# Residual and final norm weights loaded into a finished input ring, and softmax scaling by whole tiles, in the second mixer of a two-layer RWKV-7 / NSA block

## The chip, the cores and the metric

The kernel runs as one program on one core of a Trainium2 chip. The metric is device microseconds of one execution, taken as the median of several runs; lower is better. Everything is float32 outside, and matrix products are made from float32r parts (below).

## What is computed

A sequence of 256 tokens with 2048 channels goes through two layers. The first is an RWKV-7 mixer, the second a sparse-attention mixer (NSA) that reads keys and values made once from the first layer's output. Cut to what the change touches:

```python
h = h + y                                     # after the first mixer; y is its output
shared = nsa_shared_kv(h, kv_norm_g, kv_w, cmp_pe, cmp_w1, cmp_w2)
u = rmsnorm(h, b_norm_g)
proj = u @ w_in                               # 16 heads of q, 3 gates for each head, z
gates = sigmoid(gl)
s = (q . k) * d ** -0.5                       # for compressed, selected, windowed keys
p = softmax(where(visible, s, NEG_INF))       # times "any key visible" for the compressed ones
o = gb[0] * o_cmp + gb[1] * o_sel + gb[2] * o_win
h = h + (o * silu(z)) @ w_o                   # the last product, 2048 x 2048
return rmsnorm(h, final_g)
```

With 256 tokens every selected block and every windowed key is inside the causal triangle, so one head needs, for its two halves of 128 query tokens, a score tile of 128x800: 15 compressed keys and the causal keys of two kinds of key (selected and windowed).

## The kernel before, in words

**Weights.** All weight matrices stream through one class, `Weights`. SyncE (SP) loads a piece of 512 KB into one of five raw buffers (tile `wraw`, L176). ScalarE (ACT) rounds a unit of 128x512 to its high part `whi` (L204), and VectorE (DVE) subtracts to get the low part `wlo` (L189). In the last 144 units before the output projection, every third low part is made by GpSimd (POOL) instead. A product of two such numbers takes three matmuls: high by high, high by low, low by high. One raw piece holds two units, so a unit of 128x512 feeds six matmuls (L568, L569, L571) for the two halves of tokens. The high and low buffers are five deep, and the code asks for units three ahead.

**Rings.** The split input of each product lives in a ring of 16 buffers of 128x512 float32r; one buffer holds the high and the low part of 128 channels by 256 tokens. Ring `mx1` holds the normalized input `u` of the second mixer, which its query, gate and z products read. Ring `mx0` holds the attention's gated output `ob`.

**The second mixer.** `QZ` is the order in which five query blocks (`phase_q`) and sixteen z blocks (`phase_z`) of the input projection run on TensorE (PE). The last one is the z block of head 0. Beside them a generator, `attn_all`, works through the eight pairs of heads, from the last pair to the first. For a head, `weigh` makes scores on PE, adds masks, takes the maximum, takes exponentials on ACT with their sums, and scales the probabilities by gate over sum on DVE; for a pair, `attend` transposes the scaled probabilities on PE (L232 of the helper that records with a rank), splits them and multiplies them with the values. `flush` multiplies by z on POOL (L1622) and makes the two parts of `ob` (ACT L1624, POOL L1625).

**The output projection.** `phase_bo` multiplies `ob` with the last weight in column blocks of 512: `nb` = 0, 1, 2, then two blocks of 256. Block 0 takes the rows from 15 down to 0, since the pairs of heads come in that order. After each block `accumulate` adds the residual to the result (DVE L1658), squares it with a sum (ACT L1660) and multiplies it by the weights of the last norm (POOL L1661). The residual is the first layer's output, which was stored in DRAM as `hd`. Between block 0 and its `accumulate` stands `open_fin`: it releases the attention's memory (`at.release()`), and in the place of that memory it allots `fg` (1 MB, the norm's weights on all partitions) and `h2` (2 MB, the residual, tile `h` in the profile), and loads both.

**PSUM.** Block 0 of the output projection uses banks 2 and 0. From `open_fin` on the turn is 2, 3, 0, 1, so the first tile of block 1 goes to bank 2 again, which block 0's first `accumulate` has to read before.

**Order.** The code is run once as a Python generator program with a rough clock `sch.t` (a `yield` of a number lets at least that many ns of that clock go by before the generator goes on). The Tile scheduler then places instructions on each engine's queue by its own simulation. Each queue is worked off in order, so an instruction that waits holds back all behind it on its engine; SP's DMA issues are such a queue too.

Of the kernel before, what the change touches and what calls it, by code (L numbers as in the profile page):

```python
# [10 lines left out]
F32 = mybir.dt.float32  # L11
# [12 lines left out]
NCMP = 15  # L24
GRP = 4
# [190 lines left out]
def hybrid_kernel(ctx: ExitStack, tc: tile.TileContext, a: dict, out: bass.AP):  # L216
# [1165 lines left out]
    def compress(j, o):  # L1382
# [17 lines left out]
        if j == 0:  # L1400
            for m in range(2):
                PE.matmul(o2[:60, :128], hs[:, m, :], cw2[:, m, :], start=m == 0, stop=m == 1)
            kc = kvp.tile([128, 1, 1, 128], F32, name="kc", bufs=1)
            V.memset(kc, 0.0)
            S.activation(kc[:60, 0, 0, :], o2[:60, :128], AF.Copy)
            rope(kc, 1, C("ccos"), C("csin"), kvp, V)
            yield 0.0
            o3 = accp("tp")
            PE.transpose(o3[:, :60], kc[:60, 0, 0, :], ident[:60, :60])
            V.tensor_copy(KT[:, :, 0:NCMP], o3[:, :60].rearrange("p (g c) -> p g c", g=GRP))  # L1410
# [26 lines left out]
    gat = at.tile([128, 2, 48], F32, name="gat")  # L1437
    RST = at.tile([128, T], F32, name="RST")
    pr = accp("PT")
    for tt in range(2):  # L1440
# [9 lines left out]
    def phase_q(n):  # L1450
# [48 lines left out]
    def weigh(h):  # L1499
# [21 lines left out]
        vc = sc[:, 0:544].rearrange("p (x c) -> p x c", x=2)[:, :, 0:NCMP]  # L1521
        V.tensor_tensor(vA, vA, cb, op=OP.add)
        V.tensor_tensor(vc, vc, C("vis").rearrange("p (x c) -> p x c", x=2), op=OP.add)
        V.tensor_reduce(mx[:, 0, 0:2], vA, axis=AX.X, op=OP.max)
        V.tensor_reduce(mx[:, :, 2], vc, axis=AX.X, op=OP.max)
        V.tensor_tensor(vD, vD, cb, op=OP.add)
        V.tensor_reduce(mx[:, 1, 0:2], vB, axis=AX.XY, op=OP.max)
        V.tensor_scalar(mx, mx, -SCALE, None, op0=OP.mult)
        yield 500.0
        P0 = at.tile([128, 2, 128], F32, name="P0", bufs=PB)  # L1530
        P1 = at.tile([128, 2, 256], F32, name="P1", bufs=PB)
        Pc = at.tile([128, 2, 16], F32, name="Pc", bufs=2)
        Pcc = PCC[h // 2 % 2][:, h % 2]
        for x in range(2):
            S.activation(P0[:, x], vA[:, x], AF.Exp, scale=SCALE, bias=mx[:, 0, x:x + 1], accum_out=sm[:, 0, x:x + 1])
        for t in range(2):
            S.activation(Pc[:, t, 0:NCMP], vc[:, t], AF.Exp, scale=SCALE, bias=mx[:, t, 2:3], accum_out=sm[:, t, 2:3])
        for x in range(2):
            S.activation(P1[:, x].rearrange("p (s t) -> p s t", s=2), vB[:, x], AF.Exp, scale=SCALE,
                         bias=mx[:, 1, x:x + 1], accum_out=sm[:, 1, x:x + 1])  # L1540
# [5 lines left out]
        V.tensor_tensor(rc[:, :, 1], rc[:, :, 1], gv[:, :, 2], op=OP.mult)  # L1546
        V.tensor_tensor(rc[:, :, 2], rc[:, :, 2], gv[:, :, 0], op=OP.mult)
        yield 600.0
        for x in range(2):
            V.tensor_scalar(P0[:, x], P0[:, x], rc[:, 0, x:x + 1], None, op0=OP.mult)  # L1550
            V.tensor_scalar(P1[:, x], P1[:, x], rc[:, 1, x:x + 1], None, op0=OP.mult)
        for t in range(2):
            V.tensor_scalar(Pcc[:, t, 0:3, 0:NCMP], Pc[:, t, None, 0:NCMP].to_broadcast([128, 3, NCMP]),
                            rc[:, t, 2:3], None, op0=OP.mult)
# [86 lines left out]
        sch.run(phase_q(ph) if ph < 10 else phase_z(ph - 10))  # L1641

    def open_fin():
        nonlocal fg, h2, fin
# [5 lines left out]
        nc.sync.dma_start(fg, bass.AP(tensor=a["final_g"].tensor, offset=a["final_g"].offset, ap=[[0, 128], [1, D]]))  # L1650
# [3 lines left out]
    fg = h2 = fin = None  # L1654

    def accumulate(tt, ps, c0, cols, i):
        hv = h2[:, tt, c0:c0 + cols]
        V.tensor_tensor(hv, ps, hv, op=OP.add)  # L1658
# [74 lines left out]
```

## Time and profile before

| what | value |
|---|---|
| median of 3 runs | 1185.26 us (1180.89 to 1186.52) |
| the profiled execution's own time | 1179.32 us |
| span of its instructions | 1177.5 us |
| mean granted TensorE clock | 0.987 |
| busy share: PE, DVE, ACT, POOL | 95%, 73%, 60%, 30% |
| attention and input projection of the second mixer | about 849 to 1098 us |
| output projection | about 1067 to 1164 us |

The profile is of one execution. Busy times of PE are of pipelined matmuls, so a busy PE may still be issuing at less than its peak. "a <- b" in the waits means that a stood idle until b was done. Lines are those of the kernel before.

### The profile page before, as it was taken

How to read it: one execution, taken by the hardware profiler on the slowest of the kernel's cores; microseconds unless marked ns; L12 is line 12 of the kernel's file. 1: busy time of each engine (PE TensorE's matmuls, PEld its weight loads, DVE VectorE, ACT ScalarE, POOL GpSimd, SP SyncE). 2: the span in 40 equal slices, each digit the busy share in tenths (PEclk: the TensorE clock that was granted, in tenths of full speed). 3: DMA queues.
4: the chain of work that ended last, by engine and by line, in shares of the span. 5: the costliest groups of instructions: out<-in, count | busy, mean ns of one | idle time of the engine just before them, and what ended most of it. 6: DMA issues, size and time to landing. Idle time of an engine off the chain costs nothing.

```text
span 1177.5 us, 25042 instructions
## 1 busy us (share of the span) xinstructions
PE 1119.6 (95%) x9136; PEld 967.0 (82%) x9136; DVE 862.5 (73%) x1915; ACT 708.1 (60%) x1680; POOL 348.3 (30%) x437
## 2 busy tenths in 40 slices
PE   8999999999986999999989999999999999999797
PEld 6788899887966888888668888787889888888687
DVE  7999876589795886666656867674576888987464
ACT  5667877667763445554545766564656666656453
POOL 1400046234554355544010010100344434342211
PEclk9999999999997999999989999999999999999899
DMA  6559887786889769784356758585646354644652
GB/s 226 170 182 258 228 226 220 229 220 185 262 237 201 193 163 264 181 227 121 122 162 208 248 165 285 162 286 171 187 143 172 113 138 115 159 133 161 233 193 105
DMA packets 232922, 225.37 MB, mean 191 GB/s; under 512 B 51429, under 2 KB 180757, under 8 KB 232416
## 3 DMA queue, kind: packets, MB, share of 16 engines
q1 hardware_dynamic: 228000, 219.01, 62.7%
q0 software_dynamic: 4800, 4.77, 1.7%
q8 instruction: 72, 1.18, 0.4%
q14 instruction: 50, 0.41, 0.1%
HBM read 200.48 MB, written 23.10 MB: 190 GB/s over the span
## 4 chain that ended last, share of the span: by engine, by line
PE 69%; DVE 15%; issue 5%; ACT 4%; POOL 3%; DMA 3%; SPq 0%; ACTq 0%; POOLq 0%; DVEq 0%
PE bank L569 12%; PE bank L571 12%; PE bank L568 12%; PE bank L587 5%; PE bank L588 4%; DVE wlo L189 4%; PE bank L589 4%; PE bank L593 2%; PE bank L232 2%; PE bank L594 1%; PE pair L571 1%; PE pair L568 1%; ACT whi L204 1%; PE pair L569 1%; DVE invX L803 1%
## 5 line engine op out<-in xcount | busy, mean ns | idle before, releaser
L189 DVE TENSOR_TENSOR wlo<-wraw,whi 128x512 fp32r<-128x512 f32 (+2 forms) x616 | 444.3, 735 | 138.5 <-ACT whi L204 136.0
L204 ACT ACTIVATE whi<-wraw 128x512 fp32r<-128x512 f32 (+2 forms) x664 | 399.9, 620 | 186.2 <-PE bank L571 98.3
L569 PE MATMUL bank<-wlo,mx 128*128 128x512 f32 (+3 forms) x608 | 232.1, 383 | 6.4 <-DVE wlo L189 6.2
L571 PE MATMUL bank<-whi,mx 128*128 128x512 f32 (+3 forms) x608 | 229.6, 380 | 0.0
L568 PE MATMUL bank<-whi,mx 128*128 128x512 f32 (+3 forms) x608 | 205.8, 382 | 8.7 <-DVE h L1658 5.9
L587 PE MATMUL bank<-mx,whi 128*128 128x256 f32 (+1 forms) x544 | 166.1, 305 | 0.3 <-ACT mx L418 0.3
L589 PE MATMUL bank<-mx,wlo 128*128 128x256 f32 (+1 forms) x544 | 155.4, 286 | 0.4 <-DVE wlo L189 0.4
L588 PE MATMUL bank<-mx,whi 128*128 128x256 f32 (+1 forms) x544 | 155.3, 285 | 0.3 <-issue 0.3
L568 PEld LDWEIGHTS bank<-whi,mx 128*128 128x128 f32 x608 | 114.7, 190 | 28.2 <-DVE h L1658 6.3
L569 PEld LDWEIGHTS bank<-wlo,mx 128*128 128x128 f32 x608 | 115.7, 190 | 25.9 <-DVE wlo L189 8.4
L571 PEld LDWEIGHTS bank<-whi,mx 128*128 128x128 f32 x608 | 115.6, 190 | 17.9 <-POOL mx L1625 0.4
L587 PEld LDWEIGHTS bank<-mx,whi 128*128 128x128 f32 (+1 forms) x544 | 103.5, 190 | 5.7 <-ACT mx L418 0.7
L588 PEld LDWEIGHTS bank<-mx,whi 128*128 128x128 f32 (+1 forms) x544 | 103.9, 191 | 1.4 <-issue 0.5
L589 PEld LDWEIGHTS bank<-mx,wlo 128*128 128x128 f32 (+1 forms) x544 | 103.4, 190 | 1.7 <-DVE wlo L189 0.6
L189 POOL TENSOR_TENSOR wlo<-wraw,whi 128x512 fp32r<-128x512 f32 (+2 forms) x48 | 63.1, 1314 | 115.6 <-ACT whi L204 94.2
L593 PE MATMUL bank<-mx,whi 128*128 128x512 f32 x240 | 86.6, 398 | 0.0
L569 PE MATMUL bank<-wlo,kvh 128*128 128x512 f32 x192 | 77.0, 401 | 0.0
L571 PE MATMUL bank<-whi,kvl 128*128 128x512 f32 x192 | 76.1, 397 | 0.0
L594 PE MATMUL bank<-mx,wlo 128*128 128x256 f32 x256 | 70.5, 284 | 0.0
L568 PE MATMUL bank<-whi,kvh 128*128 128x512 f32 x192 | 67.5, 396 | 0.0
L418 ACT ACTIVATE mx<-mtmp 128x256 fp32r<-128x256 f32 x96 | 38.9, 412 | 26.2 <-DVE mtmp L425 25.5
L593 PEld LDWEIGHTS bank<-mx,whi 128*128 128x128 f32 x240 | 45.2, 188 | 8.8
(333 smaller groups left out, 2059.7 us busy)
## 6 DMA issues: line engine op xcount, KB each, us to landing
wraw<-in_a_w_rkvz_dram SPq DMA_DIRECT2D x128, 512.0 KB, 5.0
wraw<-in_kv_w_dram SPq DMA_DIRECT2D x48, 512.0 KB, 4.4
wraw<-in_b_w_in_dram SPq DMA_DIRECT2D x40, 512.0 KB, 4.2
wraw<-in_a_w_o_dram SPq DMA_DIRECT2D x32, 512.0 KB, 4.6
wraw<-in_b_w_o_dram SPq DMA_DIRECT2D x32, 512.0 KB, 3.7
spd<-sp SPq DMA_DIRECT2D x16, 642.0 KB, 5.1
spl<-spd SPq DMA_DIRECT2D x16, 642.0 KB, 5.4
wraw<-in_b_w_in_dram SPq DMA_DIRECT2D x24, 384.0 KB, 3.3
```

The costliest lines, as they stand in the source:

```text
L189: eng.tensor_tensor(lv, src, hv.bitcast(F32), op=OP.subtract)
L204: self.nc.scalar.activation(hv, src, AF.Copy)
L232: return fn(*args, **kw)
L418: S.activation(h, src, AF.Copy)
L568: PE.matmul(o, mh[:, ts], wh[:, 0, :], start=k == ends[0], stop=False)
L569: PE.matmul(o, mh[:, ts], wl[:, 0, :], start=False, stop=False)
L571: PE.matmul(o, ml[:, ts], wh[:, 0, :], start=False, stop=k == ends[1])
L587: PE.matmul(o, wh[:, s, :], mh, start=k == 0 and first, stop=False, **kw)
L588: PE.matmul(o, wh[:, s, :], ml, start=False, stop=False, **kw)
L589: PE.matmul(o, wl[:, s, :], mh, start=False, stop=k == NK - 1, **kw)
L593: PE.matmul(o, wh[:, s, :], joint[nm, k], start=k == 0, stop=False, **kw)
L594: PE.matmul(o[:, :T], wl[:, s, :], mh, start=False, stop=False, **kw)
```

## The change

Three things change in the second mixer; all before it stays as it was.

*The residual and the norm's weights.* `fg` and `h2` are gone. `load_tail(nb)` loads, for a column block of 512, the two token halves of `hd` and the norm's weights into three buffers of ring `mx1`, 256 KB each: 12 loads in place of two, the same 3 MB. A ring buffer is free when the last z block has read the piece of `u` in it. Nothing has to wait for the release of the attention's memory any more. `accumulate`, `finish` and the stores work in these buffers.

*The scale of the scores.* `SCALE` goes into the keys when they are written, on two instructions that existed before, so the exponentials have no scale, the maximum is taken negated at once, and the multiplication of the six maxima is dropped.

*Gates and probabilities.* The gates are stored in the order of the sums, with "any key visible" multiplied in, so four small products become one. Six scalings of a head's probabilities become three over whole tiles, each with the factors spread along the row. A `yield 2500.0` stands ahead of them.

```diff
-            S.activation(... AF.Copy)                       # kv_k: keys out of PSUM
+            S.activation(... AF.Copy, scale=SCALE)
-            V.tensor_copy(KT[:, :, 0:NCMP], o3[...])        # compress: compressed keys
+            V.tensor_scalar(KT[:, :, 0:NCMP], o3[...], SCALE, None, op0=OP.mult)
...
-                V.tensor_scalar(gat[:, tt, :], gl, 0.25, 0.25, op0=OP.mult, op1=OP.add)
+                V.tensor_scalar(gl, gl, 0.25, 0.25, op0=OP.mult, op1=OP.add)
+                g3 = gl.rearrange("p (h b) -> p h b", b=3)
+                V.tensor_copy(gat[:, tt, :, 0:2], g3[:, :, 1:3])
+                V.tensor_scalar(gat[:, tt, :, 2], g3[:, :, 0], C("anyv")[:, tt:tt + 1], None, op0=OP.mult)
...
-        V.tensor_scalar(mx, mx, -SCALE, None, op0=OP.mult)  # the maxima are now negated
...
+        yield 2500.0
         rc = at.tile([128, 2, 3], F32, name="rc", bufs=2)
         V.reciprocal(rc, sm)
-        V.tensor_tensor(rc[:, :, 2], rc[:, :, 2], C("anyv"), op=OP.mult)
-        gv = gat[:, :, h * 3:h * 3 + 3]
-        V.tensor_tensor(rc[:, :, 0], rc[:, :, 0], gv[:, :, 1], op=OP.mult)
-        V.tensor_tensor(rc[:, :, 1], rc[:, :, 1], gv[:, :, 2], op=OP.mult)
-        V.tensor_tensor(rc[:, :, 2], rc[:, :, 2], gv[:, :, 0], op=OP.mult)
+        V.tensor_tensor(rc, rc, gat[:, :, h, :], op=OP.mult)
         yield 600.0
-        for x in range(2):
-            V.tensor_scalar(P0[:, x], P0[:, x], rc[:, 0, x:x + 1], None, op0=OP.mult)
-            V.tensor_scalar(P1[:, x], P1[:, x], rc[:, 1, x:x + 1], None, op0=OP.mult)
-        for t in range(2):
-            V.tensor_scalar(Pcc[:, t, 0:3, 0:NCMP], Pc[:, t, None, 0:NCMP].to_broadcast([128, 3, NCMP]),
-                            rc[:, t, 2:3], None, op0=OP.mult)
+        V.tensor_tensor(P0, P0, rc[:, 0, 0:2, None].to_broadcast([128, 2, 128]), op=OP.mult)
+        V.tensor_tensor(P1, P1, rc[:, 1, 0:2, None].to_broadcast([128, 2, 256]), op=OP.mult)
+        V.tensor_tensor(Pcc[:, :, 0:3, 0:NCMP], Pc[:, :, None, 0:NCMP].to_broadcast([128, 2, 3, NCMP]),
+                        rc[:, :, 2:3, None].to_broadcast([128, 2, 3, NCMP]), op=OP.mult)
...
-        fg = fin.tile([128, D], F32, name="fg")             # open_fin
-        nc.sync.dma_start(fg, bass.AP(tensor=a["final_g"].tensor, ... ap=[[0, 128], [1, D]]))
-        h2 = fin.tile([128, 2, D], F32, name="h2")
-        nc.sync.dma_start(h2, hd.rearrange("(a p) c -> p a c", p=128))
+    def load_tail(nb):
+        for tt in range(3):
+            t = mixp.tile([128, 2, T], F32R, name="mx1", bufs=NK).bitcast(F32).rearrange("p a b -> p (a b)")
+            src = hd[tt * 128:(tt + 1) * 128, nb * 512:(nb + 1) * 512] if tt < 2 else \
+                bass.AP(tensor=a["final_g"].tensor, offset=a["final_g"].offset + 512 * nb, ap=[[0, 128], [1, 512]])
+            nc.sync.dma_start(t, src)
+            tail[tt, nb] = t
+    def tailed(tt, c0, cols):
+        return tail[tt, c0 // 512][:, c0 % 512:c0 % 512 + cols]
...
     def phase_bo():
+        load_tail(0)
         for nb in range(3):
+            load_tail(nb + 1)
             ps = two()
```

Where this moves instructions: first SP's queue at the end of the second mixer. The rows are DMA issues, `wraw` the raw weight pieces (of the input projection, `b_w_in`, and the output projection, `b_w_o`), `x14` so many in a row. Before:

```order
L176 DMA wraw<-in_b_w_in_dram 128x8x128 x16
L176 DMA wraw<-in_b_w_o_dram 128x2x512 x14
L1650 DMA fg<-in_final_g_dram 128x2048
L1652 DMA h_14309<-hd 128x2x2048
L176 DMA wraw<-in_b_w_o_dram 128x2x512 x10
```

Now, in SP's queue at the same place, behind the same 16 pieces of the input projection:

```order
L176 DMA wraw<-in_b_w_o_dram 128x2x512 x4
L1655 DMA mx_13919<-hd 128x512
L176 DMA wraw<-in_b_w_o_dram 128x2x512
L1655 DMA mx_13921<-hd 128x512
L1655 DMA mx_13923<-in_final_g_dram 128x512
L1655 DMA mx_13925<-hd 128x512
L1655 DMA mx_13927<-hd 128x512
L1655 DMA mx_13929<-in_final_g_dram 128x512
L1655 DMA mx_14220<-hd 128x512
L176 DMA wraw<-in_b_w_o_dram 128x2x512
L1655 DMA mx_14222<-hd 128x512
L1655 DMA mx_14224<-in_final_g_dram 128x512
```

Three more loads into the ring follow (`mx_14412`, `mx_14414`, `mx_14416`), then the other 18 pieces of that width. So the loads stand behind the 4th to 6th piece of the output projection's weights; before, they stood behind the 14th.

Second, DVE's queue at the last head of the attention (`P` are its probabilities, `pcc` those of the compressed keys, `zT` the z of another head). Before:

```order
L1482 TENSOR_REDUCE zT<-bank_14007 128x256
L189 TENSOR_TENSOR wlo<-wraw,whi 128x512
L1542 RECIPROCAL rc<-sm 128x6
L1543 TENSOR_TENSOR rc<-rc,cst 128x2
L1545 TENSOR_TENSOR rc<-rc,gat 128x2
L1546 TENSOR_TENSOR rc<-rc,gat 128x2
L1547 TENSOR_TENSOR rc<-rc,gat 128x2
L1550 TENSOR_SCALAR P_13976<-P_13976,rc 128x128
L1551 TENSOR_SCALAR P_13977<-P_13977,rc 128x256
L1550 TENSOR_SCALAR P_13976<-P_13976,rc 128x128
L1551 TENSOR_SCALAR P_13977<-P_13977,rc 128x256
L1553 TENSOR_SCALAR pcc_10950<-Pc,rc 128x3x15 x2
```

Now, on DVE for the same head:

```order
L1485 TENSOR_REDUCE zT<-bank_13792 128x256
L189 TENSOR_TENSOR wlo<-wraw,whi 128x512
L1545 RECIPROCAL rc<-sm 128x6
L1546 TENSOR_TENSOR rc<-rc,gat 128x6
L1548 TENSOR_TENSOR P_13997<-P_13997,rc 128x256
L1549 TENSOR_TENSOR P_13998<-P_13998,rc 128x512
L189 TENSOR_TENSOR wlo<-wraw,whi 128x512
L1550 TENSOR_TENSOR pcc_10950<-Pc,rc 128x2x3x15
```

Eleven instructions of the head became five, a low part of a weight now stands between two of them, and the reciprocal still follows the same two instructions.

More of the change, by code (lines that the diff above doesn't have):

```diff
@@ L1338, in kv_k @@
             S.activation(KTX[:, 2 * gp:2 * gp + 2, :, which, :],
-                         pt.rearrange("p (g s t) -> p g s t", g=2, s=2), AF.Copy)
+                         pt.rearrange("p (g s t) -> p g s t", g=2, s=2), AF.Copy, scale=SCALE)
     def kv_c(j, t):
@@ L1409, in compress @@
             PE.transpose(o3[:, :60], kc[:60, 0, 0, :], ident[:60, :60])
-            V.tensor_copy(KT[:, :, 0:NCMP], o3[:, :60].rearrange("p (g c) -> p g c", g=GRP))
+            V.tensor_scalar(KT[:, :, 0:NCMP], o3[:, :60].rearrange("p (g c) -> p g c", g=GRP), SCALE, None, op0=OP.mult)
         else:
@@ L1436, in hybrid_kernel @@
     banks(acc=(0, 1, 2), PT=(3, 4), PV=(5,))
-    gat = at.tile([128, 2, 48], F32, name="gat")
+    gat = at.tile([128, 2, HEADS, 3], F32, name="gat")
     RST = at.tile([128, T], F32, name="RST")
@@ L1523, in weigh @@
         V.tensor_tensor(vc, vc, C("vis").rearrange("p (x c) -> p x c", x=2), op=OP.add)
-        V.tensor_reduce(mx[:, 0, 0:2], vA, axis=AX.X, op=OP.max)
-        V.tensor_reduce(mx[:, :, 2], vc, axis=AX.X, op=OP.max)
+        V.tensor_reduce(mx[:, 0, 0:2], vA, axis=AX.X, op=OP.max, negate=True)
+        V.tensor_reduce(mx[:, :, 2], vc, axis=AX.X, op=OP.max, negate=True)
         V.tensor_tensor(vD, vD, cb, op=OP.add)
-        V.tensor_reduce(mx[:, 1, 0:2], vB, axis=AX.XY, op=OP.max)
-        V.tensor_scalar(mx, mx, -SCALE, None, op0=OP.mult)
+        V.tensor_reduce(mx[:, 1, 0:2], vB, axis=AX.XY, op=OP.max, negate=True)
         yield 500.0
@@ L1534, in weigh @@
         for x in range(2):
-            S.activation(P0[:, x], vA[:, x], AF.Exp, scale=SCALE, bias=mx[:, 0, x:x + 1], accum_out=sm[:, 0, x:x + 1])
+            S.activation(P0[:, x], vA[:, x], AF.Exp, bias=mx[:, 0, x:x + 1], accum_out=sm[:, 0, x:x + 1])
         for t in range(2):
-            S.activation(Pc[:, t, 0:NCMP], vc[:, t], AF.Exp, scale=SCALE, bias=mx[:, t, 2:3], accum_out=sm[:, t, 2:3])
+            S.activation(Pc[:, t, 0:NCMP], vc[:, t], AF.Exp, bias=mx[:, t, 2:3], accum_out=sm[:, t, 2:3])
         for x in range(2):
-            S.activation(P1[:, x].rearrange("p (s t) -> p s t", s=2), vB[:, x], AF.Exp, scale=SCALE,
+            S.activation(P1[:, x].rearrange("p (s t) -> p s t", s=2), vB[:, x], AF.Exp,
                          bias=mx[:, 1, x:x + 1], accum_out=sm[:, 1, x:x + 1])
+        yield 2500.0
         rc = at.tile([128, 2, 3], F32, name="rc", bufs=2)
         V.reciprocal(rc, sm)
-        V.tensor_tensor(rc[:, :, 2], rc[:, :, 2], C("anyv"), op=OP.mult)
-        gv = gat[:, :, h * 3:h * 3 + 3]
-        V.tensor_tensor(rc[:, :, 0], rc[:, :, 0], gv[:, :, 1], op=OP.mult)
-        V.tensor_tensor(rc[:, :, 1], rc[:, :, 1], gv[:, :, 2], op=OP.mult)
-        V.tensor_tensor(rc[:, :, 2], rc[:, :, 2], gv[:, :, 0], op=OP.mult)
-        yield 600.0
-        for x in range(2):
-            V.tensor_scalar(P0[:, x], P0[:, x], rc[:, 0, x:x + 1], None, op0=OP.mult)
-            V.tensor_scalar(P1[:, x], P1[:, x], rc[:, 1, x:x + 1], None, op0=OP.mult)
-        for t in range(2):
-            V.tensor_scalar(Pcc[:, t, 0:3, 0:NCMP], Pc[:, t, None, 0:NCMP].to_broadcast([128, 3, NCMP]),
-                            rc[:, t, 2:3], None, op0=OP.mult)
+        V.tensor_tensor(rc, rc, gat[:, :, h, :], op=OP.mult)
+        yield 600.0
+        V.tensor_tensor(P0, P0, rc[:, 0, 0:2, None].to_broadcast([128, 2, 128]), op=OP.mult)
+        V.tensor_tensor(P1, P1, rc[:, 1, 0:2, None].to_broadcast([128, 2, 256]), op=OP.mult)
+        V.tensor_tensor(Pcc[:, :, 0:3, 0:NCMP], Pc[:, :, None, 0:NCMP].to_broadcast([128, 2, 3, NCMP]),
+                        rc[:, :, 2:3, None].to_broadcast([128, 2, 3, NCMP]), op=OP.mult)
         yield 600.0
@@ L1643, in open_fin @@
     def open_fin():
-        nonlocal fg, h2, fin
+        nonlocal fin
         sch.require(lambda: not sch.bg)
@@ L1648, in open_fin @@
         fin = ctx.enter_context(tc.tile_pool(name="fin", bufs=1))
-        fg = fin.tile([128, D], F32, name="fg")
-        nc.sync.dma_start(fg, bass.AP(tensor=a["final_g"].tensor, offset=a["final_g"].offset, ap=[[0, 128], [1, D]]))
-        h2 = fin.tile([128, 2, D], F32, name="h2")
-        nc.sync.dma_start(h2, hd.rearrange("(a p) c -> p a c", p=128))
-    fg = h2 = fin = None
+    fin = None
+    tail = {}
+    def load_tail(nb):
[7 more added lines that the diff above has]
+        return tail[tt, c0 // 512][:, c0 % 512:c0 % 512 + cols]
     def accumulate(tt, ps, c0, cols, i):
-        hv = h2[:, tt, c0:c0 + cols]
+        hv = tailed(tt, c0, cols)
         V.tensor_tensor(hv, ps, hv, op=OP.add)
@@ L1660, in accumulate @@
         S.activation(scr[:, :cols], hv, AF.Square, accum_out=ssh[:, tt, i:i + 1])
-        (G if i < 4 else V).tensor_tensor(hv, hv, fg[:, c0:c0 + cols], op=OP.mult)
+        (G if i < 4 else V).tensor_tensor(hv, hv, tailed(2, c0, cols), op=OP.mult)
     def finish(tt):
@@ L1665, in finish @@
         for i, (c0, c1) in enumerate(((0, 512), (512, 1024), (1024, 1536), (1536, 2048))):
-            hv = h2[:, tt, c0:c1]
+            hv = tailed(tt, c0, c1 - c0)
             if i % 2:
```

## The prediction, made before the changed kernel ran

> **What bounds the kernel now.** I read the page first: PE is busy for 95% of the span and has 69% of the chain that ended last, so only time in which PE stands, or runs slowly, can be won. Then I cut the span into stages, since the change touches only what starts at about 849 us.
>
> ```profile
> PE 1119.6 (95%) x9136; PEld 967.0 (82%) x9136; DVE 862.5 (73%) x1915; ACT 708.1 (60%) x1680; POOL 348.3 (30%) x437
> ...
> PE 69%; DVE 15%; issue 5%; ACT 4%; POOL 3%; DMA 3%; SPq 0%; ACTq 0%; POOLq 0%; DVEq 0%
> ```
> ```profile
> core 0: us, PE busy (x) PEld busy (x) DVE busy (x) ACT busy (x) POOL busy (x), PEclk, DMA share, GB/s
> 849.00:1089.00 240.00, 235.12 (x1370) 209.13 (x1369) 198.58 (x509) 152.29 (x436) 92.30 (x85) 1.00 0.50 143
> 1098.40:1104.30 5.90, 0.06 (x1) 0.00 (x0) 0.69 (x2) 0.00 (x0) 0.00 (x0) 0.76 0.97 402
> 1104.30:1108.30 4.00, 3.95 (x9) 3.14 (x10) 2.20 (x3) 2.60 (x6) 2.52 (x2) 0.50 0.00 1
> 1108.30:1164.00 55.70, 55.70 (x315) 48.99 (x314) 34.51 (x49) 28.30 (x53) 7.64 (x6) 1.00 0.50 161
> ```
>
> Attention (the first stage) has PE standing for 240.0 - 235.1 = 4.9 us in all. The second is a hole: PE and ACT do nothing for 5.9 us while DMA is at 0.97. In the third, PE is busy again, with nine matmuls, but at a granted clock of 0.50. In the fourth it never stands. The waits and the chain say why the hole is there:
>
> ```profile
> DVE h L1658 <- DMA h<-hd: 6.7, 1, 6.7
> PE bank L568 <- DVE h L1658: 5.9, 1, 5.9
> ```
> ```profile
> 1092.21 1.84 POOL mx L1625 x2
> 1094.06 0.34 SPq L1650
> 1094.45 9.06 DMA h<-hd
> 1103.61 0.70 DVE h L1658
> 1104.35 0.80 PE bank L568
> ```
>
> The last pair's gated output is finished on POOL at 1094.05; only then may SP issue the loads into the attention's memory. The residual takes 9.06 us to land, `accumulate` of block 0 waits for it, and block 1 waits for `accumulate`, which has to empty bank 2. PE itself, matmul by matmul:
>
> ```profile
> 1097.39 0.39 PE L571 MATMUL bank<-whi,mx 128*128 128x512 f32 x1
> 1097.84 0.39 PE L569 MATMUL bank<-wlo,mx 128*128 128x512 f32 x1
> 1098.07 0.39 PE L571 MATMUL bank<-whi,mx 128*128 128x512 f32 x1
> 1104.35 0.80 PE L568 MATMUL bank<-whi,mx 128*128 128x512 f32 x1 [5.90 <-DVE h L1658]
> 1108.33 0.39 PE L568 MATMUL bank<-whi,mx 128*128 128x512 f32 x1
> ```
>
> Matmuls of this form start 0.23 us apart before the hole. After it the nine of the third stage lie between 1104.35 and 1108.33, 0.44 us apart in the mean.
>
> **Part 1, the loads: the hole.** With the residual in the ring before 1098, block 0's first `accumulate` starts when its last matmul ends. The first token half's last one is the row of 1097.39, which ends at 1097.78; the add takes 0.70 (the chain), so bank 2 is free at about 1098.6 with a little for signals, where the next matmul could have started at 1098.30. PE restarts at 1098.6 instead of 1104.35: **5.75 us**. DVE has no other work there (0.69 us in 5.9). A wait of 0.3 us in place of 5.9 should leave the clock at full: nine matmuls from 1104.35 to 1108.33 take 3.98 us, and nine at 0.23 take 2.07: **1.9 us**. What could be late next is the weights, and they are not: ACT stood too, so the split buffers were full before the hole, and block 1 starts on them. Behind it PE ran 55.7 us without a stand, and that pace (one piece of 512 KB for 12 matmuls, 2.8 us) stays.
>
> [...]
>
> **Part 1, the loads: what they cost where they now stand.** Each waits for the last z block to have read its ring buffer. That block's first matmul and SP's weight loads near it are these, with the ACT split that needs the 7th piece (counted along ACT's splits) and three stretches of DMA:
>
> ```profile
> 1059.05 0.39 PE L593 MATMUL bank<-mx,whi 128*128 128x512 f32 x1
> 1064.41 6.75 SPq L176 DMA_DIRECT2D wraw<-in_b_w_o_dram  x3
> 1079.91 0.63 ACT L204 ACTIVATE whi<-wraw 128x512 fp32r<-128x512 f32 x1 [0.73 <-PE bank L571]
> ```
> ```profile
> 1059.00:1066.00 7.00, 7.00 (x49) 6.45 (x48) 5.01 (x17) 4.68 (x16) 2.13 (x2) 1.00 0.24 86
> 1066.00:1079.00 13.00, 12.09 (x57) 9.78 (x56) 11.73 (x31) 9.62 (x28) 4.13 (x5) 1.00 0.46 156
> 1094.00:1105.00 11.00, 5.10 (x22) 3.90 (x21) 2.68 (x4) 1.93 (x5) 0.03 (x1) 0.84 0.86 351
> ```
>
> The z block goes by between 1059 and 1067, piece after piece, so the first loads are free to go at about 1059.5 and the last at about 1066; the 5th, 6th and 7th weight pieces (the row with x3) went at 1064.4, 1067.8 and 1070.8 anyway, waiting for raw buffers. Twelve issues at some 0.4 us each (SP's row of 0.34) are 5 us of a queue that idles. So no weight load is issued much later; but the 7th is served behind 3.1 MB of tail and up to 1.6 MB of weights. At the 351 GB/s that DMA showed with such a backlog, 4.7 MB from 1064.4 on take 13.4 us: landed at 1077.8, where ACT wants it at 1079.91. Hidden, with 2 us to spare: **0 us**. The mean agrees: 1059 to 1079 moved 0.6 + 2.0 = 2.6 MB, where 351 GB/s for 20 us would be 7.0. If the backlog moved at half that rate (176 GB/s), the piece would land at 1091 and cost up to 11 us; if all landed early, nothing. Between the ends I stand at 0, since the row of 351 is one of the same kinds of load. The tail itself lands some 20 us before it is read at 1098.
>
> **Part 2, DVE's work in attention.** The groups of that stage, mean ns of one after the comma:
>
> ```profile
> L1551 DVE TENSOR_SCALAR P<-P,rc 128x256 f32<-128x256 f32 x32 | 17.1, 533 | 0.0
> L1550 DVE TENSOR_SCALAR P<-P,rc 128x128 f32<-128x128 f32 x32 | 15.1, 471 | 0.0
> L1553 DVE TENSOR_SCALAR pcc<-Pc,rc 128x45 f32<-128x45 f32 x32 | 10.9, 380 | 0.0
> L1528 DVE TENSOR_SCALAR mx<-mx 128x6 f32<-128x6 f32 x16 | 5.2, 323 | 0.1
> L1546 DVE TENSOR_TENSOR rc<-rc,gat 128x2 f32<-128x2 f32 x16 | 3.4, 212 | 0.0
> L189 DVE TENSOR_TENSOR wlo<-wraw,whi 128x512 fp32r<-128x512 f32 x73 | 54.3, 761 | 10.8 <-ACT whi L204 10.6
> L1522 DVE TENSOR_TENSOR pair<-pair,cst 128x256 f32<-128x256 f32 x16 | 6.8, 422 | 0.2 <-PE pair L232 0.2
> ```
> ```profile
> L1551 DVE TENSOR_SCALAR P<-P,rc x32: 340/346/1408, 870.0 to 1074.3; 128x256 f32<-128x256 f32 x32
> L189 DVE TENSOR_TENSOR wlo<-wraw,whi x105: 534/680/1636, 848.4 to 1096.2; 128x512 fp32r<-128x512 f32 x73, 128x384 fp32r<-128x384 f32 x32
> ```
>
> Removed: 17.1 + 15.1 + 10.9 + 5.2, and four small products of at most 3.4 each: about 60 us. Added for each of 16 heads: one product of six numbers (0.21), the scaling of 256 (0.42, as L1522), of 512 (0.76, as L189) and of 90 numbers (between the 0.21 and the 0.42, say 0.3): 1.69 us, 27 us in all. The scalings' medians are much below their means (346 against 533 ns, up to 1408): now and then one stands until a POOL instruction is done. If each of the four new ones paid that 0.19 us, it would be 12 us more. So DVE loses **33 us, or 21**, of 198.6.
>
> [...]
>
> But DVE is not the bound. What PE lost to it is in PE's own waits from 849 to 1098, all of them:
>
> ```profile
> PE bank L232 <- DVE P L1550: 2.3, 4, 0.9
> PE bank L569 <- DVE wlo L189: 1.4, 2, 0.9
> PE bank L232 <- DVE P L1551: 0.7, 1, 0.7
> PE bank L568 <- ACT mx L1624: 0.4, 1, 0.4
> PE bank L1470 <- DVE ql L1474: 0.3, 1, 0.3
> ```
>
> Behind DVE: 2.3 + 1.4 + 0.7 + 0.3 = 4.7 us. That is the most that can be won; the least is a loss, since new places in the queues make new waits. I take 3.0 us for the waits on `P` (half of their instructions, lighter queue) less 0.5 for new ones: **2.5 us**, between 4.7 and -3 (as much lost as `P` cost before). The scale in the keys rides on two instructions that exist. Two small copies for each token half of the gates are under 1 us of DVE, once, at a point where PE has z blocks queued. The negated maximum is free.
>
> **The sum.** 5.75 + 1.9 + 0 + 2.5 = 10.2 us. The profiled execution took 1179.32 us, so it would take 1169.1; the median of the runs shown, 1185.26, is 5.9 us above it, and 10.2 below that is **1175 us**, -0.86%.
>
> **Rivals.**
> - *Attention gives nothing.* Its 2.5 us are lost to new waits, as PE is busy for 235.1 of 240 us there; the hole alone is 7.7 us: 1177.6. For it speaks that the waits are a handful of single events.
> - *The tail starves the weights.* The 4.7 MB ahead of and with the 7th piece move at two thirds of the 351 GB/s: 20.1 us, until 1084.5, 4.6 us late. PE stands in block 0 and 4.6 of the 10.2 us go back: 1179.6. Against it: the row of 351 GB/s.
> - *The hole does not close.* `accumulate` still waits for something freed late. Against it: the ring is not the attention's memory. Only part 2 is left: 1182.8.
> - *Slower: the scaling comes late to the transposes.* PE takes a head's transposes in a fixed place of its queue. The whole-tile scalings are 0.42 and 0.76 us where single ones were 0.35, and any of them can stand behind POOL for 1.4 us (the maximum above). If every head waited 1.4 us, 22.4 us would be lost: 1185.3 - 7.7 + 22.4 = 1200. It decides against the change from 7.7 / 16 = 0.48 us a head. Against it: DVE is less busy, the largest wait was 0.9 us, and the rows of the last head show as much ahead of the reciprocal as before.
>
> **Chances.** Forecast 0.52; attention gives nothing 0.22; starved weights 0.12; hole stays 0.07; slower 0.07. Faster by over 0.5% (under 1179.3; about what a measurement of this kernel can tell from no change) are the first, most of the second and some of the third: 0.73. Within 0.5%: 0.21. Slower by over 0.5%: 0.06. The range goes from all that attention could give, 5.75 + 1.9 + 4.7 = 12.4, with the 5.9 us by which the profiled execution was below the median, 1167, up to the rival that keeps only part 2, 1183. The forecast's own is 1170 to 1178.
>
> **What would show it.** After: no row "DVE ... <- DMA" at the first `accumulate` and a pause of PE under 1 us between blocks 0 and 1, at a clock of 1.00; 12 loads of 256 KB issued some 30 us before; DVE's busy time in attention near 166 us; PE's waits on `P` under 1 us in all. It would be wrong if ACT's splits wait for `wraw` between 1075 and 1095, or if the transposes collect waits on the new scalings.

## The result, and the profile after

| kernel | median, us | runs | ratio to before, 95% interval |
|---|---|---|---|
| before | 1185.05 (1180.89 to 1186.52) | 4 | |
| changed | 1170.84 (1165.64 to 1174.15) | 4 | 0.9882 [0.9836, 0.9927] |
| changed, measured again | 1168.95 (before: 1184.25) | 4 | 0.9879 [0.9864, 0.9894] |

The change makes the kernel 1.2% faster, 14.2 us between the medians. The forecast was 1175 us, in a range of 1167 to 1183. The profiled execution of the changed kernel took 1169.41 us with a span of 1167.3 us, 10.2 us less than the profiled execution of before.

The page's line of engines, and its line of the chain that ended last:

```profile
PE 1117.6 (96%) x9136; PEld 966.6 (83%) x9136; DVE 858.8 (74%) x1807; ACT 707.6 (61%) x1680; POOL 349.7 (30%) x437
...
PE 71%; DVE 14%; issue 4%; ACT 4%; DMA 4%; POOL 3%; SPq 0%; ACTq 0%; POOLq 0%; DVEq 0%
```

PE's share rose from 95% to 96%. DVE issues 108 instructions less and is busy for only 3.7 us less (862.5 before). The stages, cut at the places that answer to those of before:

```profile
core 0: us, PE busy (x) PEld busy (x) DVE busy (x) ACT busy (x) POOL busy (x), PEclk, DMA share, GB/s
849.00:1087.00 238.00, 235.56 (x1384) 210.90 (x1383) 196.05 (x401) 153.69 (x438) 93.54 (x86) 1.00 0.56 160
1087.00:1097.00 10.00, 9.60 (x41) 7.07 (x40) 4.07 (x7) 5.72 (x12) 6.09 (x6) 1.00 0.40 141
1100.00:1155.00 55.00, 55.00 (x320) 48.80 (x319) 33.79 (x49) 27.06 (x53) 7.98 (x6) 1.00 0.49 159
```

The hole and the half clock behind it are gone: 1087 to 1097 holds the end of block 0 and the start of block 1, at a clock of 1.00, and PE stands there for 0.40 us, inside block 0. The two blocks meet in the next rows of PE. The first two of the three matmuls at 1092.50 are the last of block 0, one for each token half, and the third is of block 1 already (`warm_hole` below shows this). On DVE the first `accumulate` starts 0.15 us after the first of them has ended (1092.50 + 0.39), and PE doesn't stop:

```profile
1092.27 0.40 PE L569 MATMUL bank<-wlo,mx 128*128 128x512 f32 x1
1092.50 0.85 PE L571 MATMUL bank<-whi,mx 128*128 128x512 f32 x3
```
```profile
1093.04 1.28 DVE L1663 TENSOR_TENSOR mx<-bank,mx 128x512 f32<-128x512 f32 x2
```

Two rows that each profile has mark the stretch that the change touches: the first start of `L593` (the first z product) and the last start of `L571` (one of the last products of the output projection). They are the two numbers ahead of the forms. Before, then changed:

```profile
L593 PE MATMUL bank<-mx,whi x240: 387/395/484, 848.7 to 1066.3; 128*128 128x512 f32 x120
L571 PE MATMUL bank<-whi,mx x608: 283/389/629, 17.5 to 1158.0; 128*128 128x512 f32 x112, 128*128 128x384 f32 x24, 128*128 128x432 f32 x8, 128*128 128x256 f32 x8
```
```profile
L593 PE MATMUL bank<-mx,whi x240: 387/395/481, 850.7 to 1065.3; 128*128 128x512 f32 x120
L571 PE MATMUL bank<-whi,mx x608: 283/389/632, 17.8 to 1147.4; 128*128 128x512 f32 x112, 128*128 128x384 f32 x24, 128*128 128x432 f32 x8, 128*128 128x256 f32 x8
```

From mark to mark the kernel before took 1158.0 - 848.7 = 309.3 us, the changed one 1147.4 - 850.7 = 296.7: **12.6 us** less. Of that 2.0 us went into a longer time ahead of the first mark, which no kernel of this study changes (it ended between 848.7 and 855.3 us in all their profiles), and 0.4 into the end. So the profiled execution of before was the quickest of all up to the first mark, and the stretch between the marks, called *marked stretch* from here, is the better measure of a cause:

| kernel | marked stretch, us | median, us | ratio, 95% interval | weight loads' waits, us |
|---|---|---|---|---|
| before | 309.3 | | | 10.6 |
| changed; again | 296.7; 296.6 | 1170.84; 1168.95 | 0.9882; 0.9879 | 6.5; 6.4 |
| loads_only | 301.0 | 1174.18 | 0.9915 [0.9901, 0.9928] | 10.6 |
| scale_only | 305.3 | 1177.73 | 0.9948 [0.9936, 0.9961] | 6.2 |
| warm_hole | 307.7 | 1180.89 | 0.9970 [0.9958, 0.9982] | 10.7 |
| traffic | 299.3 | 1174.33 | 0.9923 [0.9900, 0.9946] | 7.4 |
| no_yield | 298.8 | 1172.91 | 0.9914 [0.9892, 0.9935] | 6.4 |
| scale_ts; again | 292.2; 291.3 | 1164.43; 1166.39 | 0.9847 [0.9824, 0.9870]; 0.9851 [0.9832, 0.9869] | 0.4; 0.4 |
| ts_six | 296.1 | 1170.50 | 0.9886 [0.9872, 0.9900] | 5.8 |
| apool0 | 293.4 | 1168.35 | 0.9873 [0.9853, 0.9893] | 2.2 |
| ts_apool0 | 293.2 | 1167.61 | 0.9873 [0.9852, 0.9895] | 2.2 |
| before_apool0 | 311.3 | 1187.30 | 1.0029 [1.0018, 1.0041] | 13.1 |

The last column sums the rows "PEld ... <- ..." of the waits from 849 us to the end of the attention and block 0. What it is good for is told below. The kernels of one group of runs share a median of before: 1184.25 us for loads_only to warm_hole and the second measurement, 1182.4 for no_yield, scale_ts, apool0 and traffic, 1183.8 for the others.

### The profile page after: what moved, and what is told of

It is laid out like the page before. It is cut to its first block, busy times and chain, and to the rows that moved or that the text cites. A ratio compares the mean times of both kernels' runs of the same rounds, so it can differ in the third digit from the quotient of the medians.

```text
span 1167.3 us, 24959 instructions
## 1 busy us (share of the span) xinstructions
PE 1117.6 (96%) x9136; PEld 966.6 (83%) x9136; DVE 858.8 (74%) x1807; ACT 707.6 (61%) x1680; POOL 349.7 (30%) x437
## 4 chain that ended last, share of the span: by engine, by line
PE 71%; DVE 14%; issue 4%; ACT 4%; DMA 4%; POOL 3%; SPq 0%; ACTq 0%; POOLq 0%; DVEq 0%
PE bank L569 12%; PE bank L571 12%; PE bank L568 12%; PE bank L587 5%; DVE wlo L189 5%; PE bank L593 4%; PE bank L588 4%; PE bank L589 4%; PE bank L594 2%; PE bank L232 2%; PE pair L571 1%; PE pair L568 1%; PE pair L569 1%; ACT whi L204 1%; DMA wraw<-in_a_w_rkvz_dram 1%
## 5 line engine op out<-in xcount | busy, mean ns | idle before, releaser
L189 DVE TENSOR_TENSOR wlo<-wraw,whi 128x512 fp32r<-128x512 f32 (+2 forms) x616 | 452.0, 749 | 139.8 <-ACT whi L204 138.3
L571 PE MATMUL bank<-whi,mx 128*128 128x512 f32 (+3 forms) x608 | 228.7, 379 | 0.0
L571 PEld LDWEIGHTS bank<-whi,mx 128*128 128x128 f32 x608 | 115.1, 189 | 17.7 <-POOL mx L1622 0.4
L593 PE MATMUL bank<-mx,whi 128*128 128x512 f32 x240 | 86.8, 398 | 0.0
L571 PE MATMUL bank<-whi,kvl 128*128 128x512 f32 x192 | 76.1, 396 | 0.0
L593 PEld LDWEIGHTS bank<-mx,whi 128*128 128x128 f32 x240 | 45.1, 188 | 8.7
```

Source lines behind the costliest of these rows:

```text
L189: eng.tensor_tensor(lv, src, hv.bitcast(F32), op=OP.subtract)
L571: PE.matmul(o, ml[:, ts], wh[:, 0, :], start=False, stop=k == ends[1])
L593: PE.matmul(o, wh[:, s, :], joint[nm, k], start=k == 0, stop=False, **kw)
```

## The experiments

**Each part alone.** `loads_only` is the kernel before with `load_tail` and `tailed` in place of `fg` and `h2`; `scale_only` is the kernel before with all other edits of the change (scale in the keys, negated maxima, ordered gates, three scalings, the `yield`).

> Only the first part of the change: the residual and the norm's weights go into the ring; scaling, gates and keys as before. Hole theory: this part is worth the hole and the slow clock behind it, 5.75 + 1.9 = 7.7 us, so 0.65% faster than before, and the trace shows no wait of the first accumulate on a DMA, a pause of PE under 1 us between blocks 0 and 1 and a granted clock of 1.00 there, while PE's waits on P in attention stay near the 3.0 us of before. Rival (the lighter DVE queue is at least half of the gain of 14 us between the medians): 3 to 6 us, and something else, a weight that lands late, takes part of the hole's worth back.

> Only the second part: scaling by whole tiles, gates ordered, scale in the keys, with the yield; residual and norm's weights loaded as before. Hole theory: 2 to 3 us faster (0.2%), the hole of 5.9 us with its DMA wait and the stretch at half clock still there, PE's waits on P under 1 us. Rival: 6 us or more faster (0.5%). DVE's busy time falls by only some 3 us, not by 21 or 33, if what POOL holds up is only handed on to other instructions.

> The changed kernel again, beside its two parts on one chip. Hole theory: its gain is the sum of the two parts, 10 us (0.86%). Rival: the parts overlap or help each other, and the sum of the two gains differs from the whole by more than 4 us.

The marked stretch fell by 8.3 us with the loads alone and by 4.0 us with the scalings alone. Their sum, 12.3, comes close to the 12.6 of the whole change: the parts add up and neither hides the other. Both gave more than was expected of them, 7.7 and 2 to 3 us. By the ratio of its runs `scale_only` is even 6.2 us faster (4.6 to 7.6), as much as its rival asked for; over all kernels of the table the gain between the medians lies between 1.9 us below and 2.6 us above that of the marked stretch. PE's waits on `P` are the same rows as before in the first, and the hole is the same pair of rows in the second. loads_only, then scale_only:

```profile
PE bank L232 <- DVE P L1550: 2.3, 4, 0.9
PE bank L569 <- DVE wlo L189: 1.4, 2, 0.9
```
```profile
DVE h L1655 <- DMA h<-hd: 7.0, 1, 7.0
...
PE bank L568 <- DVE h L1655: 6.1, 1, 6.1
```

**The clock behind the hole.** `warm_hole` is the kernel before with 46 products of 256 columns that stand in the code between block 0 and block 1 and go into a bank that nothing reads. The residual still comes late.

```diff
+                wm = psum.tile([128, 512], F32, name="bank5", bufs=1)
+                for i in range(46):
+                    PE.matmul(wm[:, :T], mixed[("ob", 0)][1][:, 0:128], mixed[("ob", 0)][0], start=True, stop=True)
```

> The kernel before with 46 extra products of 128x256 on TensorE behind block 0's last matmul, into a bank that nothing reads, some 5.4 us of work that only fills the hole. Hole theory: the loads land when they did and block 1 starts no earlier, but at full clock, so only the clock's 1.9 us are won (0.16%) and the row of 4.0 us at a clock of 0.50 is gone. Rival (the half speed behind the hole is not of the idle time but of the DMA burst or of cold buffers): the nine matmuls stay 0.44 us apart and the time is that of before or up to 1 us longer.

PE's timeline from the end of block 0 on:

```profile
1098.36 0.62 PE L571 MATMUL bank<-whi,mx 128*128 128x512 f32 x2
1098.82 5.67 PE L1680 MATMUL bank<-mx 128*128 128x256 f32 x46
1104.32 0.40 PE L571 MATMUL bank<-whi,mx 128*128 128x512 f32 x1
1104.56 0.40 PE L568 MATMUL bank<-whi,mx 128*128 128x512 f32 x1
...
1108.13 0.50 PE L568 MATMUL bank<-whi,mx 128*128 128x512 f32 x1 [0.68 <-DVE h L1658]
1108.47 0.39 PE L569 MATMUL bank<-wlo,mx 128*128 128x512 f32 x1
```

The products show where block 0 ends: two `L571` stand ahead of them and one behind. In the kernel before the same three are one row, and they lie well ahead of the hole:

```profile
1094.89 0.84 PE L571 MATMUL bank<-whi,mx 128*128 128x512 f32 x3
```

So PE was in block 1 already when the hole came. The blocks behind block 0 have 4 x 96 = 384 matmuls, and 369 stand behind the hole, so 15 were done: three for each of the five units that the split buffers hold, which can only be those of the token half that doesn't need bank 2.

The products fill the hole, and behind them PE goes on 0.23 us apart, where the nine behind the hole of before were 0.44 apart. The marked stretch is 1.6 us shorter, although bank 2 came free 0.4 us later, counted from the first mark; the median is 3.4 us shorter (2.1 to 5.0 by the interval of the ratio). So the slow stretch behind the hole is an effect of PE standing, and not of the loads, which still came late here; it costs about what the prediction said, 1.9 us. The wait of 0.68 us that is left in block 1 does not slow what comes behind it.

**The margin of the weights.** `traffic` is the changed kernel with each of the 12 tail loads issued a second time, into the same buffers.

```diff
+        for nb in range(4):
+            load_tail(nb)
+        for t, src in again:
+            nc.sync.dma_start(t, src)
```

> The changed kernel with each of the 12 loads into the ring issued a second time into the same buffer, 3.1 MB more ahead of and among the 7th and 8th weight pieces of the output projection. If the margin of the weights is the 1 to 2 us that the changed kernel's trace shows (7th piece landed at 1076.5, split at 1077.5), ACT now waits for weight pieces and PE stands 3 to 6 us in block 0: 3 to 6 us slower than the changed kernel. Rival (raw buffers and split buffers hold enough): within 1 us of it, and no wait of ACT on a weight DMA there.

First the changed kernel: SP's first and last tail load and the issue of the 7th weight piece (the first of the five), then what the DMA view says of that issue alone (us to landing at the end), then ACT's split that needs it:

```profile
1058.40 0.34 SPq L1655 DMA_DIRECT2D mx<-hd  x1
...
1067.65 0.42 SPq L1655 DMA_DIRECT2D mx<-in_final_g_dram  x1
1069.64 8.57 SPq L176 DMA_DIRECT2D wraw<-in_b_w_o_dram  x5
```
```profile
wraw<-in_b_w_o_dram SPq DMA_DIRECT2D x1, 512.0 KB, 6.9
```
```profile
1077.53 0.63 ACT L204 ACTIVATE whi<-wraw 128x512 fp32r<-128x512 f32 x1 [0.73 <-PE bank L571]
```

The piece landed at 1069.64 + 6.9 = 1076.5, and ACT began at 1077.53, released by PE and not by the load: 1.0 us to spare. With the loads doubled, ACT waits for it, in two rows of the waits:

```profile
ACT whi L204 <- DMA wraw<-in_b_w_o_dram: 6.8, 2, 5.3
...
PE bank L568 <- ACT mx L1621: 1.8, 1, 1.8
```
```profile
1076.00:1084.00 8.00, 8.00 (x40) 6.53 (x39) 2.51 (x5) 1.94 (x5) 0.00 (x0) 1.00 1.02 348
1084.00:1100.00 16.00, 14.18 (x60) 11.31 (x59) 7.69 (x13) 7.84 (x17) 5.65 (x6) 0.89 0.71 263
```

ACT stood for 6.8 us, yet PE has the splits made ahead to live on and stands only later, for 1.8 us, when ACT makes the last pair's part of `ob` late; the clock falls behind that, to a mean of 0.89 in this row. The marked stretch is 2.6 us longer than the changed kernel's, and by the ratios the kernel is some 5 us slower, where 3 to 6 were expected. So the rival "the tail starves the weights" is a real mechanism which 3 MB more bring about. In the changed kernel ACT is 1.0 us from waiting for a weight, and PE some more from feeling it.

**What the scalings do.** Three variants of the changed kernel. `no_yield` leaves out `yield 2500.0`. `scale_ts` keeps everything but the scaling of `P`, which is done by four scalar multiplications again; `scale_ts_again` is its second measurement. `ts_six` takes back the scaling of the compressed keys' probabilities too.

```diff
-        V.tensor_tensor(P0, P0, rc[:, 0, 0:2, None].to_broadcast([128, 2, 128]), op=OP.mult)
-        V.tensor_tensor(P1, P1, rc[:, 1, 0:2, None].to_broadcast([128, 2, 256]), op=OP.mult)
+        for x in range(2):
+            V.tensor_scalar(P0[:, x], P0[:, x], rc[:, 0, x:x + 1], None, op0=OP.mult)
+            V.tensor_scalar(P1[:, x], P1[:, x], rc[:, 1, x:x + 1], None, op0=OP.mult)
```

> The changed kernel without the yield of 2500 ahead of the reciprocal. If fewer and larger DVE instructions took away PE's waits on P, they stay under 1 us here too and the time is that of the changed kernel within 2 us. Rival (the later place of the scaling took them away): waits on P return, 2 to 3 us, and the time is 2 to 3 us longer than the changed kernel's.

> The changed kernel with the four scalings of P0 and P1 by a scalar for each half, as before, in place of two whole-tile products; the rest of the change stays. If the kind of instruction mattered (each scaling by a scalar standing behind POOL once in a while), PE's waits on P return to 1 to 3 us and DVE's busy time in attention rises by 2 to 5 us. Rival (what POOL holds up is handed from one instruction to another, whatever its kind): DVE's busy time within 2 us of the changed kernel's, the scalings slow and the weights' low parts quicker. The time within 3 us of the changed kernel's by both.

> The changed kernel with P0 and P1 scaled by a scalar for each half, again, now beside the others. If the four smaller instructions are really better than the two whole-tile products, it is again 1.3 to 1.7% faster than before and the first z product to the last product of the program take near 304 us, as in its first run (changed kernel 308). Rival (the first run's lead was chance): 1.0 to 1.3% faster, as the changed kernel.

> As scale_ts, with the compressed keys' scaling too in two instructions by a scalar: all six as before the change, with the ordered gates, the scale in the keys and the yield. If an instruction of one tensor and a scalar stands behind POOL less or ends sooner, DVE's busy time after 849 us falls below scale_ts's 234.8 us and the time is equal or up to 3 us less. Rival (what counts is the number of instructions): 1 to 3 us more.

Without the `yield` PE's waits on `P` do not come back, but one on `wlo` of 1.8 us is there (0.9 in the changed kernel, on POOL) and the marked stretch is 2.1 us longer. Most of that stands in no row of a wait: behind the stand of 1.8 us the clock fell to half (columns as in the table of stages).

```profile
996.60:1000.20 3.60, 3.60 (x12) 3.60 (x13) 3.46 (x9) 0.93 (x4) 0.00 (x0) 0.53 0.73 189
1000.20:1004.00 3.80, 3.80 (x24) 3.66 (x22) 3.23 (x8) 3.60 (x15) 1.06 (x1) 1.00 0.76 188
```

At 0.53 for 3.6 us PE loses some 1.7 us, an estimate from the first row.

`scale_ts` is the best kernel of the study, twice: 0.9847 and 0.9851, some 4 us quicker than the changed kernel, with a marked stretch of 292.2 and 291.3 us. From 849 to 1087 PE does not stand at all:

```profile
849.00:1087.00 238.00, 238.00 (x1406) 215.43 (x1405) 190.55 (x435) 158.98 (x443) 96.31 (x88) 1.00 0.56 163
```

DVE issues 34 instructions more in this window than in the changed kernel and is busy for 5.5 us less, where 2 to 5 us more or a difference within 2 us were expected. The scalings themselves did not get shorter: their rows go from 20.4 us (two products a head) to 30.4 (four). What got shorter are others, the low parts of 128x512 (mean 856 to 776 ns) and the product for the compressed keys. Changed, then `scale_ts`:

```profile
L1550 DVE TENSOR_TENSOR pcc<-Pc,rc 128x90 f32<-128x90 f32 x16 | 10.4, 650 | 0.0
```
```profile
L1551 DVE TENSOR_TENSOR pcc<-Pc,rc 128x90 f32<-128x90 f32 x16 | 3.9, 242 | 0.0
```

`ts_six` has nearly the same DVE time (190.98) and none of the lead; it was expected to be at most 3 us slower than `scale_ts` and is 4 to 5 us slower in the marked stretch. What differs is where PE waits: 5.8 us at its weight loads against 0.4. Which order of the queues makes that difference was not tried.

Neither `no_yield` nor `ts_six` has a wait of a PE matmul on `P`. So neither the `yield` nor the whole-tile scaling is needed for these waits to go, and which edit of part 2 took them away is not shown.

**POOL beside DVE.** A constant of the program, `APOOL`, gives POOL a share of the low parts `wlo` in the second mixer. At 0, DVE makes all of them. `apool0` sets it in the changed kernel, `ts_apool0` in `scale_ts`, `before_apool0` in the kernel before.

```diff
-APOOL = 3
+APOOL = 0
```

> The changed kernel with no low part of a weight on POOL: the 48 that POOL made go to DVE. Theory of the handed-on wait: DVE's low parts of 128x512 fall from a mean of 859 ns to under 740 and the six-number and 90-number products to their shortest times; the 48 more cost DVE 48 x 0.6 = 29 us, and some 20 to 30 us of standing behind POOL go, so DVE's busy time in attention changes by less than 10 us. Rival (the slow instructions are slow by themselves): DVE's busy time rises by about 29 us. Time: within 5 us of the changed kernel's, since PE is the bound.

> scale_ts with no low part of a weight on POOL. If both gains come from DVE standing less behind POOL, they overlap, and this is within 2 us of scale_ts. Rival (two separate gains): 2 to 4 us faster than scale_ts.

> The kernel before, with no low part of a weight on POOL and nothing else changed. Theory of the handed-on wait: DVE gets 48 instructions more and stands less, so its busy time after 849 us stays within 10 us of 242.7; the scalings of 256 numbers fall from a mean of 533 ns to under 400, PE's waits on P from 3.0 us to under 1.5, and the time falls by 0 to 4 us. Rival (the scalings are slow by their own, and POOL's help is needed): DVE busy near 270 us and the time longer than before's.

The stage of `apool0`, which answers to the row of 849 to 1087 above:

```profile
849.00:1087.00 238.00, 237.56 (x1402) 214.83 (x1400) 198.32 (x447) 159.04 (x443) 38.92 (x44) 1.00 0.56 163
```

POOL's busy time falls by 54.6 us. DVE takes 46 instructions more, most of them low parts of 0.6 us or more, and its busy time rises by 2.3 us. At 0.6 us each, 46 more would have cost 27.6 us. So what POOL took off DVE in the changed kernel, DVE paid back by standing behind POOL. The marked stretch is 3.3 us shorter; the median shows no gain over the changed kernel that the intervals would bear out. With `scale_ts` it adds nothing: 293.2 us where `scale_ts` alone has 292.2 and 291.3. Nor do the four scalings of `scale_ts` make a difference to DVE any more when POOL makes no low parts. `ts_apool0`:

```profile
849.00:1087.00 238.00, 237.55 (x1402) 214.93 (x1400) 198.19 (x479) 159.58 (x443) 36.28 (x44) 1.00 0.58 165
```

In the kernel before it makes the scalings of 256 quicker as well (mean 533 to 377 ns), and the time 0.3% longer, since waits on ACT (`Th` 2.9 us, `mx` 3.6) come in the place of those on `P`. That miss shows that DVE's load is not by itself what PE waits for.

## Why the prediction was right, and which of its sizes were off

**The hole: right, and slightly small.** 5.75 + 1.9 = 7.65 us were forecast, and the loads alone gave 8.3 in the marked stretch. The `accumulate` of block 0 finds its residual there, no row "DVE ... <- DMA" is left, and the clock stays at 1.00. `warm_hole` shows the 1.9 us apart from the 5.75. Of the 0.7 us between 7.65 and 8.3, 0.3 are the wait for bank 2 that the prediction left in, with PE back at 1098.6 and not at 1098.30: the rows above show no wait at all. It took the rows of 1097.39 and 1098.07 for the last of block 0, but they are of block 1. Block 0's first half was done at 1094.89 + 0.39 = 1095.28; with its residual there, `accumulate` would have emptied bank 2 at about 1096 (an estimate from these rows), before PE needed it at 1098.30. The other 0.4 us are not traced. The attention itself is untouched there: loads_only has 10.6 us of waits at the weight loads, as before.

**The loads where they now stand: right at 0, with less room than said.** Landed at 1077.8 with 2 us to spare was the estimate; 1076.5 with 1.0 us it was, as attention itself ran earlier. The row of 351 GB/s was the right one: from 1066 to 1079 the changed kernel moved 347 GB/s at a share of 0.99.

**DVE's busy time: wrong by six to nine times.** The step that failed is the sum "about 60 us" less 27 (or less 39): DVE was to lose 33 us (or 21) and lost 3.7 over the whole kernel (862.5 before, 858.8 now). From 849 to 1087 the difference is 1.4 (197.41 before, 196.05 now), but the changed kernel does more of its work in that window. Two readings failed in the sum.

First, durations of small instructions overlap, and the prediction added them up. The first head's scalings, before and now:

```profile
869.26 0.19 DVE L1542 RECIPROCAL rc<-sm 128x6 f32<-128x6 f32 x1 [2.29 <-ACT P L1539]
869.48 0.17 DVE L1543 TENSOR_TENSOR rc<-rc,cst 128x2 f32<-128x2 f32 x1
869.56 0.15 DVE L1545 TENSOR_TENSOR rc<-rc,gat 128x2 f32<-128x2 f32 x1
...
871.01 0.68 DVE L189 TENSOR_TENSOR wlo<-wraw,whi 128x512 fp32r<-128x512 f32 x1
```
```profile
869.76 0.19 DVE L1545 RECIPROCAL rc<-sm 128x6 f32<-128x6 f32 x1 [1.96 <-ACT P L1541]
869.99 0.17 DVE L1546 TENSOR_TENSOR rc<-rc,gat 128x6 f32<-128x6 f32 x1
870.19 0.42 DVE L1548 TENSOR_TENSOR P<-P,rc 128x256 f32<-128x256 f32 x1
870.53 0.68 DVE L1549 TENSOR_TENSOR P<-P,rc 128x512 f32<-128x512 f32 x1
871.13 0.25 DVE L1550 TENSOR_TENSOR pcc<-Pc,rc 128x90 f32<-128x90 f32 x1
871.29 3.59 DVE L189 TENSOR_TENSOR wlo<-wraw,whi 128x512 fp32r<-128x512 f32 x4
```

By the starts, a head took 871.01 - 869.26 = 1.75 us before and 871.29 - 869.76 = 1.53 now. The product of 0.17 us starts 0.08 us ahead of the next: half of it lies under its successor. Sixteen heads save 16 x 0.22 = 3.5 us by the starts, and not 33; the multiplication of the maxima, also in the sum, starts 0.07 us ahead of its successor where nothing holds it, which is 1 us more. In these rows the products overlap whose successor doesn't read their result (0.17 us long, 0.08 to the next start). Where it does, as at 869.99 in the changed kernel, nothing overlaps: 0.17 us, and 0.20 to the next start.

Second, the means held DVE's standing behind POOL, and that was handed to other instructions. In the last row above four low parts take 3.59 us, while POOL has one of 1.62 us at work from 871.51. The second of the four makes the difference: it starts at 871.90 and takes 1.78 us, to 0.55 us after the end of POOL's at 873.13, where the others take 0.68 or 0.69. Where POOL has none, four take 2.49:

```profile
1072.92 2.49 DVE L189 TENSOR_TENSOR wlo<-wraw,whi 128x512 fp32r<-128x512 f32 x4
```

Over attention the low parts' mean rose from 761 to 859 ns, which for 73 of them is 7.1 us, and the products of 512 that replaced scalings took 803 ns, with a median of 685. `apool0` confirms it: with POOL's low parts gone these two means are 732 and 684.

**The whole-tile scalings saved DVE next to nothing.** The prediction went by the means. By the medians of before two scalings of 256 take 2 x 346 = 692 ns, and one product of 512, a low part, takes 680. With POOL's low parts out of the way, DVE is busy for 198.32 us with two products a head (`apool0`) and for 198.19 with four scalings by a scalar (`ts_apool0`). The 5.5 us of `scale_ts` are another thing: there other instructions stand less behind POOL (the means of 856 to 776 and 650 to 242 ns above). Attention did gain (4.0 us in scale_only), without DVE saving much.

**Attention's gain: right in sign, small in size, and its cap was wrong.** 2.5 us were forecast and 4.0 came (scale_only), with PE's waits on `P` gone as said. The reason given, a lighter queue of DVE, is not what the runs show, since the queue was hardly lighter; that the sign came out is in part luck. And the prediction called 4.7 us "the most that can be won", from PE's waits behind DVE, and `scale_ts` wins 301.0 - 291.75 = 9.3 us over loads_only, which differs from it in part 2 alone (and `scale_ts` has only a form of that). The view to read was that of the weight loads. A matmul's record here is 0.39 us long, and they start 0.23 us apart, so PE can issue up to 0.16 us late without standing in its record, and each wait is short by as much (an estimate from these two numbers). PE's weight loads, 0.19 us long at the same spacing, show the wait almost whole. Before, then in `scale_ts`:

```profile
PEld bank L232 <- DVE P L1550: 3.7, 6, 1.1
PEld bank L569 <- DVE wlo L189: 2.2, 3, 1.1
PEld bank L568 <- ACT mx L1624: 1.2, 2, 0.8
PEld bank L232 <- DVE P L1551: 0.9, 1, 0.9
...
```
```profile
PEld bank L569 <- DVE wlo L189: 0.2, 1, 0.2
PEld bank L1473 <- ACT whi L204: 0.2, 1, 0.2
```

All such rows before make 10.6 us, and the last column of the table has the sum for each kernel. Among the kernels without the hole it goes with the marked stretch almost one to one: 10.6 and 301.0, 6.5 and 296.7, 5.8 and 296.1, 2.2 and 293.4, 0.4 and 292.2 or 291.3. From the first to the last 10.2 us of waits went, and 9.3 us of time (by the mean of the two). `before_apool0` follows it on the other side: 2.5 us more of waits than before, 2.0 us more of time. `no_yield` is off that line by some 2 us and `traffic` by 1.7. In both the clock fell behind a stand of 1.8 us, and that is worth as much: 1.7 us in the row of `no_yield`, and 0.11 x 16.0 = 1.8 us in that of `traffic` (estimates from these rows).

**The rivals.** "The hole does not close" and "slower" are excluded by the rows above: the largest wait of PE on a scaling is gone, not grown to 0.48 us a head. "Attention gives nothing" is excluded by scale_only, 0.9948 [0.9936, 0.9961].

**The median.** The forecast took its sum, 10.2 us, off the median and gave 1175. The stretch that the change touches gave 12.6, 2.4 more. The other 1.6 us of the 14.2 are within the interval of the ratio, which reaches from 8.6 to 19.4 us. That the spans of the two profiled executions differ by just the forecast's 10.2 us is chance: 12.6 were won between the marks and 2.4 lost outside them.

## What to carry to other kernels

Price a group of small instructions by the starts of its members where nothing disturbs them, and never by adding up mean durations: here these overlapped (0.17 us long, 0.08 apart) and held waits that other instructions took over (the low parts' mean rose from 761 to 859 ns). For what a busy TensorE loses to others, sum the waits of its weight loads; the matmuls' own waits gave half of it here (5.1 of 10.6 us in the kernel before). A load that is used late belongs into memory that is free early, but count what it goes ahead of in the DMA queue: here 1.0 us was left.

## What the runs showed of the hardware

- POOL's low parts cost DVE nearly what they save it: without them (`apool0`) 54.6 us of POOL's time are gone, DVE has 46 instructions more, and 2.3 us more of busy time. Where the two engines met, DVE's low part lasted until 0.55 us after POOL's (1.78 us against 0.68), and four took 3.59 us against 2.49.
- The length of a stand of PE alone does not say whether the clock falls. Behind a stand of 1.8 us it fell in `traffic` (0.89 from 1084 to 1100) and in `no_yield` (0.53 for 3.6 us). Behind one of 2.0 us in `apool0` it stayed at 1.00, in `before_apool0` the mean is 1.00 from 849 to 1087 with one of 2.7 us in it, and behind 0.68 us in `warm_hole` the matmuls kept their 0.23 to 0.34 us. The row of `apool0`, to compare with that of `traffic`:

```profile
1084.00:1100.00 16.00, 14.00 (x66) 11.53 (x65) 7.62 (x12) 8.69 (x17) 5.50 (x6) 1.00 0.29 100
```
